# Zero-tile products around the first modulation group, and a mixer head's weights in smaller background pieces

## The chip, the cores and the metric

The kernel runs on one core of a Trainium2 chip. A core has five engines, each with its own in-order instruction queue: TensorE (PE, matrix products; PEld is its weight load), VectorE (DVE), ScalarE (ACT), GpSimd (POOL) and SyncE (SP, which here only issues transfers). The metric is the device time of one execution in microseconds, the median of several runs; lower is better.

## The reference, cut to what matters

Two layers over 256 latent tokens and 256 context tokens of width 1024. Layer 0 mixes tokens with a bidirectional mLSTM of four heads, layer 1 with latent attention; each is followed by a gated ConvFFN. Every sub-layer is modulated by columns computed from a condition vector, and ends in a LayerNorm.

```python
def _modulation(cond, w, b):
    m = jax.nn.silu(cond) @ w + b
    return jnp.split(m[:, None, :], 6, axis=-1)
...
        # one head, one chunk of the mLSTM scan
        wmat = jnp.exp(dmat - mj[..., None]) * jnp.einsum("bhjd,bhsd->bhjs", qc, kc)
        den = g * jnp.einsum("bhjd,bhd->bhj", qc, n) + jnp.sum(wmat, -1)
        h = num / jnp.maximum(jnp.abs(den), jnp.exp(-mj))[..., None]
...
    hl = _modulate(x, ml[0], ml[1])
    x = _layer_norm(ALPHA * x + ml[2] * yl, ln_g[i, 0], ln_b[i, 0])
    f = _conv_ffn(_modulate(x, ml[3], ml[4]), ...)
    x = _layer_norm(ALPHA * x + ml[5] * f, ln_g[i, 1], ln_b[i, 1])
```

## The kernel before

**Numbers in two halves.** Every fp32 operand is split into a rounded high half and the remainder, and a product is three matmuls (`mm3`, lines 383 to 385: high by high, high by low, low by high). For weights, ACT writes the high half (line 323) and DVE the low half (line 326); for activations it is lines 388 and 389. The weights stream from HBM in tiles of 128x1024 (512 KB): three buffers `raw` for what has landed, three buffers `w` for the two halves (`NRAW`, `NB`, line 32). `raw` is free for the next transfer when both halves have been written; `w` is free when the last product that reads it is done.

**The start.** `start_up` (line 584) computes the first two modulation vectors in four groups of 256 columns, interleaved with the first projection `up`. The order on PE, DVE and ACT is written out by hand in `STEPS` (line 50) and kept as it stands. `S` splits a group's modulation weights (four tiles for a group), `A` multiplies them with the condition (`ada_rows`, line 462: 16 products of 512 columns for a group, four for a tile, in the order high, low, high, low; one PSUM row `adar`), then ACT copies the row out (line 477), `T` transposes it (line 484), `M` applies it, `W` splits a tile of `up`, two digits are products of `up`. `D` issues products of a tile of zeros (`self.zero`, line 435) into a PSUM tile `idle` that nothing reads (line 659): three after `A0`, six after `T0`.

**The heads.** For head h the main line issues the query and key projection (`w_qk`, line 921: eight weight tiles, 24 products each), then `av(h-1)`, the product of the finished mixing weights with the values, then the scores `s_mm(h)`. Beside it runs background work as Python generators: every weight tile is followed by `tick`, which advances the first generator in the list by one step for each tick (two after each tile here, so 16 in a head). `post(h-2)` (line 1098) is first in the list: it squares, normalises (line 1107) and transposes (`hnT`, line 1113) the head before. `head(h-1)` (line 963) is next: masks, then for three groups of query blocks the exponentials on ACT (line 1007), their product with the scores on DVE (line 1008), the denominators `R` (1014 to 1018), and the scaled and added weights `W` (1023, 1025), then three steps of transposes `PT` (line 1037). Each of the three groups is one step. At the seventh of the eight tiles `v_load` issues the next values' transfers on POOL's queue.

**The last head** is computed beside the output projection `mout`: eight weight tiles (12 products `y` each, two ticks each), with `head(3)` and then `post(2)` as background and the values of head 3 split along the way; then `av(3)`, then the rest of `mout`. A second background list multiplies modulation weights on DVE (`junk`, line 512), with a rate of its own.

Outside `start_up` a scheduler places the instructions of each engine by the program order and its own estimate of when they can run. So a step that is issued later in Python can move other instructions too; the order that comes out is read from the built program, engine by engine.

**The end.** `ln_rows` (line 1131) normalises the two halves of the latent tokens; `nm` (line 1151) is minus the mean times the reciprocal deviation, a bias for ACT.

Of the kernel before, what the change touches and what calls it, by code (L numbers as in the profile page):

```python
# [11 lines left out]
ALU = mybir.AluOpType  # L12
# [35 lines left out]
GROUPS = ((0, 2), (2, 4), (4, 6), (6, 8))  # L48
LOADS = [(c[0], int(c[1])) for c in "a0 r0 r1 x0 r2 a1 r3 r4 x1 a2 x2 x3 a3".split()]
STEPS = [(c[0], int(c[1])) for c in (  # L50
    "S0 W0 A0 D3 T0 D6 M0 W1 W2 S1 00 01 W3 W4 A1 03 T1 M1 02 04 10 11 S2 A2 12 T2 M2 13 14 21 "
    "S3 20 A3 24 T3 22 23 M3 31 32 33 34 30").split()]

TAIL = {"mout": 4, "aout": 7, "fout1": 6}
# [300 lines left out]
class K:  # L355
# [106 lines left out]
    def ada_rows(self, g, parts):  # L462

        nc = self.nc
        f0, f1 = GROUPS[g]
        nf = f1 - f0
        n = 256 * nf
        pr = self.ps("adar")
        for i, (hi, lo) in enumerate(parts):
            for kk in range(1024 // n):  # L470
                k = i * (1024 // n) + kk
                c = slice(kk * n, (kk + 1) * n)
                for x in (hi, lo):
                    nc.tensor.matmul(pr[0:4, :n], self.condr[:, k, :], x[:, c], start=k == 0 and x is hi,
                                     stop=k == 7 and x is lo)
        r = self.s2("adarow")
        nc.scalar.copy(r[0:4, :n], pr[0:4, :n])
        return r
# [105 lines left out]
    def start_up(self):  # L584

        nc, st = self.nc, self.st
        self.hT = []
        self.xcd = self.dr.tile([16, 128, 512], F32, name="xcd")
        self.xmd = self.dr.tile([16, 128, 512], F32, name="xmd")
        self.t2d = {(n, p, j): self.dr.tile([128, 1024], F32, name="t2d")  # L590
                    for n, a, b in (("v", 2, 4), ("y", 1, 6)) for p in range(a) for j in range(b)}
        self.xA, self.x1, self.xc, self.xcr = {}, {}, [], []
        w, ps, raws = [], [], []
        src = self.a["ada_w"][0]
        self.adaw, self.xT = {}, []
        for op, g in LOADS:
            f0, f1 = GROUPS[g] if op != "r" else (0, 0)
            if op == "a":
                wd = 128 * (f1 - f0)
                nk = 512 // wd  # L600
                self.adaw[g] = []
                for k in range(8):
                    if k % nk == 0:
                        t = self.uf("adaw")
                        self.adaw[g].append(t)
                    ap = bass.AP(tensor=src.tensor, offset=src.offset + k * 128 * 6 * D + f0 * 128,
                                 ap=[[6 * D, 128], [D, 2], [1, wd]])
                    c = k % nk * 2 * wd
                    nc.sync.dma_start(t[:, c:c + 2 * wd].rearrange("p (a b) -> p a b", a=2), ap)
            elif op == "x":  # L610
                for i in range(f0, f1):
                    x = self.s2("xT")
                    nc.sync.dma_start(x, self.a["tokT"][i])
                    self.xT.append(x)
            else:
                n, _ = st.ids["up", g, 0]
                r = self.pool.tile([128, 1024], F32, tag="raw" if g < 3 else "ar", name="raw0",
                                   bufs=NRAW if g < 3 else 2)
                nc.sync.dma_start(r, st.ws[n])
                raws.append(r)  # L620

        def wsplit(m):
            if m < 3:
                t = self.pool.tile([128, 2, CW], F32R, tag="w", name="w", bufs=NB)
                h, l = t[:, 0], t[:, 1]
            elif m == 3:
                h, l = [self.pool.tile([128, CW], F32R, tag="acc", name="w0", bufs=2) for _ in range(2)]
            else:
                h, l = [self.pool.tile([128, CW], F32R, tag="u", name="w0", bufs=NU) for _ in range(2)]
            self.split(h, l, raws[m])  # L630
            w.append((h, l))
            ps.append(self.ps("up"))

        def part(g, ms):
            for m in ms:
                for k in range(*GROUPS[g]):
                    c = slice(k * 128, (k + 1) * 128)
                    self.mm3(ps[m], (w[m][0][:, c], w[m][1][:, c]), (self.hT[k][:, 0], self.hT[k][:, 1]),
                             k == 0, k == 7)

        e = mybir.EngineType
        idle = self.ps("idle")
        rows = {}
        with self.tc.manual_schedule(engines={e.PE, e.DVE, e.Activation}):
            for op, g in STEPS:
                if op == "S":
                    rows[g] = self.ada_split(g)
                elif op == "A":
                    rows[g] = self.ada_rows(g, rows[g])
                elif op == "T":  # L650
                    rows[g] = self.ada_T(g, rows[g])
                elif op == "M":
                    self.ada_cols(g, rows.pop(g))
                    self.mod_tiles(range(*GROUPS[g]))
                elif op == "W":
                    wsplit(g)
                elif op == "D":
                    for _ in range(g):
                        nc.tensor.matmul(idle, self.zero[:, 0:128], self.zero, start=True, stop=True)
                else:  # L660
                    part(int(op), [g])
        for m in range(NUP):
            self.up_evac(m, ps[m])
# [299 lines left out]
    def head(self, h, S, big=False):  # L963
        nc = self.nc
# [11 lines left out]
        for g in range(3):  # L976
# [7 lines left out]
            nd = len(jbs)  # L984
            rng = {}
            for i, t in enumerate(jbs):
                base = 256 * i if g == 0 else 0
                for d in range(2):
                    o = W[d]
                    bias = self.gcol[:, 0, t, 32 * d + h:32 * d + h + 1]  # L990
                    spans = [(t * 128, (t + 1) * 128, Am[d])]
                    if d == 0:
                        if t > 0:
                            spans.append((0, t * 128, aB[d]))
                        lo, hi = 0, (t + 1) * 128
                    else:
                        if t == 0:
                            spans.append((128, 256, aB[d]))
                        if t >= 2:
                            spans.append((0, 256, aB[d]))  # L1000
                        if t == 2:
                            spans.append((384, 512, aB[d]))
                        lo, hi = {0: (0, 256), 1: (128, 256), 2: (0, 512), 3: (0, 512)}[t]
                    if d == 1 and t == 3:
                        nc.vector.memset(o[:, 256:384], 0.0)
                    for s0, s1, src in spans:
                        nc.scalar.activation(o[:, base + s0:base + s1], src[:, s0:s1], AF.Exp, bias=bias, scale=1.0)
                    nc.vector.scalar_tensor_tensor(o[:, base + lo:base + hi], o[:, base + lo:base + hi], 1.0,
                                                   S[g][:, base + lo:base + hi], op0=ALU.mult, op1=ALU.mult,
                                                   accum_out=den[:, 2 * i + d:2 * i + d + 1])  # L1010
                    rng[i, d] = (base + lo, base + hi)
            dv = den[:, 0:2 * nd]
            R = self.tiny(4, "R")
            nc.vector.scalar_tensor_tensor(R[:, 0:2 * nd], dv, -1.0, dv, op0=ALU.mult, op1=ALU.max)
# [4 lines left out]
            for i, t in enumerate(jbs):  # L1019
# [4 lines left out]
                                        op0=ALU.mult)  # L1024
                nc.vector.scalar_tensor_tensor(W[big][:, s0:s1], W[1 - big][:, s0:s1],
                                               R[:, 2 * i + 1 - big:2 * i + 2 - big], W[big][:, s0:s1],
                                               op0=ALU.mult, op1=ALU.add)
# [103 lines left out]
    def ln_rows(self, pss, xres, gate, fin=None):  # L1131

        nc = self.nc
        self.zs = zs = []
        for t in range(2):
            z = self.uf("z")
            st = self.tiny(6 * len(pss[t]), "st").rearrange("p (a b) -> p a b", b=6)
            for i, (ps, c) in enumerate(pss[t]):
# [4 lines left out]
                                               op0=ALU.mult, op1=ALU.add)  # L1143
                nc.vector.bn_stats(st[:, i], z[:, c])
            mv = self.tiny(2, "mv")
            nc.vector.bn_aggr(mv, st)
            rs = self.tiny(1, "rs")
            nc.scalar.activation(rs, mv[:, 1:2], AF.Sqrt, bias=self.keps, scale=1.0)
            nc.vector.reciprocal(rs, rs)
            nm = self.tiny(1, "nm")  # L1150
            nc.vector.scalar_tensor_tensor(nm, mv[:, 0:1], -1.0, rs, op0=ALU.mult, op1=ALU.mult)
            fine = len(pss[1]) > 2
            if fin is not None:
                g, b, out = fin
                for c0, c1 in ((0, 512), (512, 1024)):
                    c, h = slice(c0, c1), c0 // 512
                    hc = slice(c0 - h * 512, c1 - h * 512)
                    if t or c0 == 512:
                        nc.vector.scalar_tensor_tensor(z[:, c], z[:, c], mv[:, 0:1], g[h][:, hc],
                                                       op0=ALU.subtract, op1=ALU.mult)  # L1160
# [823 lines left out]
```

## Time and profile before

| | us |
|---|---|
| runs (three) | 1384.81, 1385.51, 1386.47 |
| median | 1385.51 |
| the profiled execution, its whole time | 1386.22 |
| its span, first to last instruction | 1384.1 |
| DVE busy in the span | 1090.0 (79%) |
| ACT busy | 713.1 (52%) |
| weight loads (PEld) busy | 1123.2 (81%) |
| 16 DMA engines moved | 297.58 MB, 215 GB/s on average |

The profile is one execution. Its page gives totals; its other views give the instructions in order of time (start, duration, engine, line, operation, tiles, and in brackets how long the engine had idled and what ended that), the waits summed by who waited for whom, and the busy time of each engine in chosen stretches, with the clock that TensorE was granted (PEclk, 1.00 is full). A matmul's duration includes its way through the array, so products that follow each other closely start more often than their durations say.

### The profile page before, as it was taken

The numbers are of one execution on the slowest core, as the hardware profiler recorded it, in microseconds if no ns is written. First come the engines' busy times: TensorE is split into PE (matmuls) and PEld (weight loads), VectorE is DVE, ScalarE is ACT, GpSimd is POOL, SyncE is SP. The second block draws the span as 40 slices with busy tenths as digits, with TensorE's granted clock in tenths as the row PEclk, the third lists the DMA queues.
The fourth block names the chain that finished last, engine by engine and source line by source line (L and its number), as shares of the span: only waits on it lengthen the run. The fifth ranks groups of instructions, "written<-read, shape, count | busy, mean of one in ns | idle before, by whom it ended". The sixth has DMA issues, their size and how long they took to land.

```text
span 1384.1 us, 18592 instructions
## 1 busy us (share of the span) xinstructions
PE 1354.0 (98%) x6567; PEld 1123.2 (81%) x6567; DVE 1090.0 (79%) x1768; ACT 713.1 (52%) x1221; POOL 121.6 (9%) x215
## 2 busy tenths in 40 slices
PE   7999999999999999999999999999999999999997
PEld 3788888888788888878898888888777888888886
DVE  6598857687688697779799878668898789788873
ACT  6585534435444555364643434334637567466660
POOL 0033000011011011120002000000001001000100
PEclk9999999999999999999999999999999999999999
DMA  9689847789666364766747877646987425256750
GB/s 338 227 293 316 290 156 247 239 286 302 214 200 204 105 232 132 250 193 228 241 147 239 300 230 234 212 145 229 312 231 226 137 99 202 109 185 185 252 202 31
DMA packets 97900, 297.58 MB, mean 215 GB/s; under 512 B 12136, under 2 KB 24808, under 8 KB 97808
## 3 DMA queue, kind: packets, MB, share of 16 engines
q1 hardware_dynamic: 68672, 218.52, 47.5%
q0 software_dynamic: 17472, 57.57, 13.3%
q10 hardware_dynamic: 11664, 20.32, 4.1%
q8 instruction: 51, 0.84, 0.2%
q14 instruction: 41, 0.34, 0.1%
HBM read 262.90 MB, written 33.46 MB: 214 GB/s over the span
## 4 chain that ended last, share of the span: by engine, by line
PE 91%; DVE 5%; ACT 2%; issue 1%; DMA 0%; SPq 0%; DVEq 0%; ACTq 0%
PE fin L1320 9%; PE fin L383 6%; PE fin L384 6%; PE fin L385 6%; PE tok L383 6%; PE tok L384 6%; PE tok L385 6%; PE y L384 5%; PE y L385 5%; PE y L383 5%; PE qk L383 4%; PE qk L385 4%; PE qk L384 4%; PE up L383 2%; PE up L385 2%; PE up L384 2%
## 5 line engine op out<-in xcount | busy, mean ns | idle before, releaser
L326 DVE TENSOR_TENSOR w<-raw,w 128x1024 fp32r<-128x1024 f32 (+3 forms) x290 | 348.1, 1203 | 141.3 <-ACT w L323 140.3
L323 ACT CAST w<-raw 128x1024 fp32r<-128x1024 f32 (+3 forms) x290 | 300.4, 1037 | 306.2 <-PE tok L385 88.6
L512 DVE SCALAR_TENSOR_TENSOR junk<-ar,bc 128x1024 f32<-128x1024 f32 x128 | 156.0, 1218 | 4.9 <-ACT bc L554 2.1
L384 PE MATMUL fin<-h,w 128*128 128x512 f32 (+1 forms) x376 | 141.2, 376 | 0.0
L385 PE MATMUL fin<-h,w 128*128 128x512 f32 (+1 forms) x376 | 140.9, 375 | 0.0
L383 PE MATMUL fin<-h,w 128*128 128x512 f32 (+1 forms) x376 | 140.8, 376 | 0.1
L1320 PE MATMUL fin<-h,w 128*128 128x256 f32 (+1 forms) x640 | 113.0, 339 | 0.0
L1320 PEld LDWEIGHTS fin<-h,w 128*128 128x128 f32 x640 | 98.2, 189 | 14.7
L383 PE MATMUL qk<-xc,w 128*128 128x512 f32 x256 | 100.7, 393 | 0.0
L385 PE MATMUL qk<-xc,w 128*128 128x512 f32 x256 | 99.9, 390 | 0.0
L384 PE MATMUL qk<-xc,w 128*128 128x512 f32 x256 | 99.8, 390 | 0.0
L384 PEld LDWEIGHTS fin<-h,w 128*128 128x128 f32 x376 | 70.8, 188 | 12.9 <-DVE h L1212 0.2
L385 PEld LDWEIGHTS fin<-h,w 128*128 128x128 f32 x376 | 70.8, 188 | 12.9
L383 PEld LDWEIGHTS fin<-h,w 128*128 128x128 f32 x376 | 70.5, 188 | 13.1 <-ACT h L1211 0.3
L383 PEld LDWEIGHTS qk<-xc,w 128*128 128x128 f32 x256 | 48.1, 188 | 10.0 <-issue 0.4
L385 PEld LDWEIGHTS qk<-xc,w 128*128 128x128 f32 x256 | 48.1, 188 | 9.9
L384 PEld LDWEIGHTS qk<-xc,w 128*128 128x128 f32 x256 | 48.1, 188 | 9.7
L383 PE MATMUL up<-hT,w 128*128 128x512 f32 x128 | 50.5, 394 | 0.5 <-ACT hT L388 0.5
L384 PE MATMUL up<-hT,w 128*128 128x512 f32 x128 | 50.1, 392 | 0.5 <-DVE hT L389 0.5
L385 PE MATMUL up<-hT,w 128*128 128x512 f32 x128 | 50.1, 391 | 0.3 <-DVE w L389 0.3
L383 PE MATMUL tok<-w,hT 128*128 128x512 f32 x128 | 49.8, 389 | 0.0
L384 PE MATMUL tok<-w,hT 128*128 128x512 f32 x128 | 49.8, 389 | 0.0
(463 smaller groups left out, 3151.2 us busy)
## 6 DMA issues: line engine op xcount, KB each, us to landing
raw<-in_ws SPq DMA_DIRECT2D x287, 512.0 KB, 4.3
ar<-in_adaT SPq DMA_DIRECT2D x80, 512.0 KB, 4.6
adaw<-in_ada_w SPq DMA_DIRECT2D x32, 256.0 KB, 6.7
t2d<-raw ACTq DMA_DIRECT2D x13, 512.0 KB, 4.9
raw<-t2d SPq DMA_DIRECT2D x13, 512.0 KB, 6.3
raw<-in_ws POOLq DMA_DIRECT2D x13, 512.0 KB, 8.0
zr<-fd ACTq DMA_DIRECT2D x33, 128.0 KB, 3.9
xmd<-xr POOLq DMA_DIRECT2D x16, 256.0 KB, 5.0
```

The costliest lines, as they stand in the source:

```text
L323: k.nc.scalar.copy(h[:, :cols], src)
L326: k.nc.vector.tensor_sub(l[:, :cols], src, h[:, :cols])
L383: mm(out, w[0], x[0], start=start, stop=False)
L384: mm(out, w[0], x[1], start=False, stop=False)
L385: mm(out, w[1], x[0], start=False, stop=stop)
L512: nc.vector.scalar_tensor_tensor(o, w, 1.0, self.bc[j], op0=ALU.mult, op1=ALU.mult, accum_out=col[:, k, j:j + 1])
L1320: nc.tensor.matmul(o, a, b, start=k == 0 and i == 0, stop=k == 7 and i == 1)
```

## The change

Three edits.

1. In the hand-written order, nine zero products are put ahead of `S0`, and in group 0's `ada_rows` two more ahead of the second, third and fourth weight tile: 15 more products in all.
2. `head` yields more often: after each of the two blocks of the first group but the last, and between a group's products (line 1008) and its denominators. A head has 12 yields and not 8; the transposes are its steps 10 to 12 and not 6 to 8.
3. `nm` is left out where the final LayerNorm does not use it (the second token tile).

In the built programs PE has 15 more instructions, DVE one fewer, the other engines as many as before. Positions move only in `w_qk` of heads 1 to 3 and in the first part of `mout`: `PT` of a head comes two weight tiles later, and on DVE and ACT the weight halves stand in other places among the head's steps. In the first part of `mout` DVE's list before `post`'s scaling (line 1107) changes from the weight tiles 3, 4, 5 and 6 to the tiles 3 to 9, and from no `junk` product to two; on PE the sixteen `hnT` transposes come after tile 7's products and no longer among tile 6's, and five of tile 8's products come ahead of `av(3)`. POOL's and SP's instructions are the same, with other waits on buffers, and some modulation loads stand a place earlier on SP.

```diff
@@ STEPS
-    "S0 W0 A0 D3 T0 D6 M0 W1 W2 S1 00 01 W3 W4 A1 03 T1 M1 02 04 10 11 S2 A2 12 T2 M2 13 14 21 "
+    "D9 S0 W0 A0 D3 T0 D6 M0 W1 W2 S1 00 01 W3 W4 A1 03 T1 M1 02 04 10 11 S2 A2 12 T2 M2 13 14 21 "
@@ ada_rows
         for i, (hi, lo) in enumerate(parts):
+            if g == 0 and i:
+                for _ in range(2):
+                    nc.tensor.matmul(self.idle, self.zero[:, 0:128], self.zero, start=True, stop=True)
             for kk in range(1024 // n):
@@ start_up
-        idle = self.ps("idle")
+        idle = self.idle = self.ps("idle")
@@ head
                     rng[i, d] = (base + lo, base + hi)
+                if i < nd - 1:
+                    yield
+            yield
             dv = den[:, 0:2 * nd]
@@ ln_rows
-            nm = self.tiny(1, "nm")
-            nc.vector.scalar_tensor_tensor(nm, mv[:, 0:1], -1.0, rs, op0=ALU.mult, op1=ALU.mult)
+            if fin is None or t == 0:
+                nm = self.tiny(1, "nm")
+                nc.vector.scalar_tensor_tensor(nm, mv[:, 0:1], -1.0, rs, op0=ALU.mult, op1=ALU.mult)
```

## The prediction

> **What bounds the kernel now.** I read the page, then the stretches, then each place the change touches in order of time.
>
> ```profile
> span 1384.1 us, 18592 instructions
> PE 1354.0 (98%) x6567; PEld 1123.2 (81%) x6567; DVE 1090.0 (79%) x1768; ACT 713.1 (52%) x1221; POOL 121.6 (9%) x215
> ...
> raw<-in_ws SPq DMA_DIRECT2D x287, 512.0 KB, 4.3
> ```
> ```profile
> 490.00:550.00 60.00, 59.98 (x284) 49.85 (x283) 47.67 (x98) 30.85 (x68) 5.77 (x11) 1.00 0.52 175
> ...
> 590.00:620.00 30.00, 28.81 (x142) 23.34 (x141) 23.26 (x58) 23.03 (x49) 6.63 (x13) 1.00 0.60 187
> 620.00:640.00 20.00, 20.00 (x98) 16.74 (x97) 19.37 (x30) 10.94 (x21) 0.00 (x0) 1.00 0.67 223
> ```
>
> Columns of the stretches: length, then busy PE, PEld, DVE, ACT, POOL, then clock. PE sets the end: 98% busy, and all of 620 to 640. So a hole opened in PE ahead of such a stretch is paid in full. Heads 1 to 3 (490 to 550 is one) leave PE no hole to close. The first part of `mout` leaves 1.19 us (30.00 less 28.81); almost all of it is this wait, for tile 4's low half:
>
> ```profile
> 605.47 1.22 DVE L326 TENSOR_TENSOR w<-raw,w 128x1024 fp32r<-128x1024 f32 x1
> ...
> 606.74 0.50 PE L384 MATMUL y<-w,hn 128*128 128x512 f32 x1 [1.07 <-DVE w L326]
> ```
>
> The most this edit can give is therefore 1.07 us.
>
> **Zero products.** The start in order:
>
> ```profile
> 0.95 0.48 DVE L436 MEMSET zero<- 128x512 f32 x1
> ...
> 6.79 0.59 PE L474 MATMUL adar<-adas,condr 128*4 128x512 f32 x1 [6.79 <-ACT adas L388]
> ...
> 8.05 1.87 PE L474 MATMUL adar<-adas,condr 128*4 128x512 f32 x4 [0.67 <-DVE adas L389]
> ...
> 10.12 2.56 PE L474 MATMUL adar<-adas,condr 128*4 128x512 f32 x8 [0.20 <-DVE adas L389]
> ...
> 13.01 0.86 PE L474 MATMUL adar<-adas,condr 128*4 128x512 f32 x3 [0.33 <-DVE adas L389]
> ...
> 13.71 0.85 PE L659 MATMUL idle<-zero 128*128 128x512 f32 x3
> ...
> 15.38 0.60 ACT L572 ACTIVATE xT<-xT,mod 128x256 f32<-128x256 f32 x1 [0.90 <-DVE mod L495]
> ```
> ```profile
> 18.30 1.99 ACT L388 CAST w<-raw 128x1024 fp32r<-128x1024 f32 x2
> 20.20 3.89 ACT L388 CAST adas<-adaw 128x1024 fp32r<-128x1024 f32 x4
> 23.99 1.99 ACT L388 CAST w<-raw 128x1024 fp32r<-128x1024 f32 x2
> ```
>
> At 8.05 products start every (1.87 - 0.59) / 3 = 0.43 us, at 13.01 every (13.71 - 13.01) / 3 = 0.23. The pace doubles inside the row at 10.12. The group's last burst runs at full pace already and begins when DVE delivers the last low half. So earlier warmth has nothing left to speed up here; and after 15.38 ACT's list is nearly solid to 26, so whatever delays the group's end delays all.
>
> When is the pace full? The two drops in the profile tell:
>
> ```profile
> 4.29:7.70 3.41, 0.59 (x1) 1.00 0.97 308
> 7.70:11.11 3.41, 2.86 (x7) 1.00 1.03 380
> ...
> 605.03:608.45 3.42, 2.35 (x11) 1.00 0.95 288
> 1076.07:1079.48 3.41, 1.81 (x12) 1.00 0.00 0
> 1079.48:1082.90 3.42, 3.42 (x14) 0.50 0.00 0
> ...
> 1185.30:1188.71 3.41, 1.46 (x11) 1.00 0.00 0
> 1188.71:1192.12 3.41, 3.35 (x15) 0.50 0.00 0
> ```
>
> (Length, PE busy, clock.) Both drops last 3.41 us and start 109.23 = 32 x 3.413 apart: windows that run free. Counted back, 313 of them from 1079.48 end at 11.1, where the pace doubles. A window with 1.81 or 1.46 us busy is followed by half clock, one with 2.35 or 2.86 by full, one with 0.59 leaves it cold. (The early 1.00 is then a missing record.)
>
> The nine products start at 1.5, when the zeros are written, and fill the window to 4.29 (2.8 of 3.41): full clock from there. They end near 5, and PE waits for the same data as before until 6.79, with one product, then 8.05. The window to 7.70 has under 1 us of work, less than the 1.46 that lost the clock: cold again from 7.70. From 8.05 PE has 15 real and six zero products. To 11.11 it starts (11.11 - 8.05) / 0.43 = 7, the other 14 take 3.2: end 14.3, against 13.01 + 3 x 0.23 = 13.7. Cost 0.6. As the windows run free, other executions have the boundary elsewhere: at 10.2 the same sum gives 13.9, at 13.0 it gives 15.2, so +0.2 to +1.5. I take +0.6. If the clock held, the zeros would fit into PE's waits, for 0.
>
> The Trainium skill (TensorE: Matmul & The Clock Gate, "What's actually happening") gives such a free-running window of about 3.4 us, and has the clock fall "after ≥1 idle window". Read literally, a window with some work would keep the clock, and the cost would be 0; this trace disagrees, with drops after 1.46 and 1.81 us of work.
>
> **Heads 1 to 3.** `PT` of heads 1 and 2 now ends right ahead of `av`.
>
> ```profile
> 512.18 1.28 DVE L389 TENSOR_TENSOR PT<-PT 128x512 fp32r<-128x512 f32 x2
> ...
> 522.35 0.69 DVE L389 TENSOR_TENSOR qk<-qk 128x512 fp32r<-128x512 f32 x1 [1.12 <-ACT qk L388]
> ```
>
> `av` begins with the first `PT` group, ready a tile earlier: 12 products, 2.7 us at 0.23. In that time ACT casts a weight tile (about 1.0) and two `PT`, DVE does one weight half and the two `PT` (1.28): about 3.6 us after the tile's end, when the second group is first read at 0.9 (eight transposes) + 2.7 = 3.6. DVE had 1.12 us idle here. I take 0; two misses, each of one such `PT` row (1.28), are the upper end, and there is no hole to gain.
>
> **The first part of `mout`.** Here DVE is the second bound:
>
> ```profile
> 597.20:615.50 18.30, 18.05 (x51) 1.00 0.71 222
> ```
> ```profile
> 613.89 1.67 DVE L1107 TENSOR_SCALAR oh<-oh,ss 128x512 f32<-128x512 f32 x4
> ...
> 614.60 2.00 PE L1113 MATMUL hnT<-ident,oh 128*128 128x128 f32 x16
> ...
> 615.48 1.22 DVE L512 SCALAR_TENSOR_TENSOR junk<-ar,bc 128x1024 f32<-128x1024 f32 x1
> 616.62 1.22 DVE L326 TENSOR_TENSOR w<-raw,w 128x1024 fp32r<-128x1024 f32 x1
> ...
> 620.11 0.39 PE L383 MATMUL av<-v,PT 128*128 128x512 f32 x1
> ```
>
> Length, DVE busy: 18.05 of 18.30 us up to the end of `post`'s scaling. Tile 4's low half moves ahead of most of the head and the 1.07 us go. But three more weight halves and two `junk` now stand ahead of the scaling, each as long as the next other, 1.14 from start to start (615.48 to 616.62): 5.7 us. With no idle left but 0.25, the scaling moves from 613.89-615.5 to 619.3-621.0. PE, in order, needs it for `hnT`. What PE does before `hnT` is all of 593 to 620.11 less the transposes (1.8) and less the old hole: it is there at 620.1 - 1.8 - 1.07 = 617.2. It waits from 617.2, first for over 2 us, then at the pace of the scaling, and ends the transposes near 621.0 + 0.6 = 621.6: 1.5 later than before. That is the lower bound of the walk. The upper one has the weights' arrival in it: tile 9's `raw` buffer is tile 6's, whose low half is now done near 611; plus 4.3 to land, 1.0 to cast, and two `PT` casts behind it on ACT whose low halves DVE does before tiles 8 and 9: scaling to 622.1, transposes to 622.6, 2.5 later. I take +2.2, nearer to that end, since the transfers' 4.3 us is itself a row. Nothing later gives it back, PE being full. Outside the walk the price runs from -1.1 (no new wait) to +3.5 (`junk`'s own load late too).
>
> A wait of over 2 us and transposes at half density leave 3 to 4 us idle within 5; split over two windows that is at least 1.5 in one, about the 1.6 (3.41 - 1.81) that dropped the clock. So a cold window follows, of which PE can use two thirds: 3.41 x 2/3 x 1/2 = +1.1 (0 to 1.7).
>
> **The end.**
>
> ```profile
> 1379.38 0.15 DVE L1151 SCALAR_TENSOR_TENSOR nm<-mv,rs 128x1 f32<-128x1 f32 x1
> 1379.45 1.41 DVE L1161 SCALAR_TENSOR_TENSOR z<-z,rs,br 128x512 f32<-128x512 f32 x2
> ```
>
> `nm` stands alone on the path: -0.07.
>
> **Sum.** 0.6 + 0 + 2.2 + 1.1 - 0.07 = +3.8 on the profiled execution (span 1384.1, whole 1386.22): 1390.0. That execution lies 0.7 above the median 1385.51, so I forecast 1389.3.
>
> **Rivals.**
>
> - *The finer steps only free tile 4* (not slower). Place: DVE's list in `mout`; it decides if the scaling still ends before PE has used up tile 7, that is, if DVE does its list some 4 us faster than its rows say. The wait of 1.07 goes, the zeros cost nothing: 1385.5 - 1.1 - 0.1 = 1384.3. Against it: 18.05 busy of 18.30. Chance 0.12.
> - *The clock holds* through windows with a little work: no 0.6 and no 1.1, leaving 2.2 - 0.07 = +2.1: 1387.6. For it: 2.35 us of 3.42 were enough at 605; against it: the two drops. Chance 0.18. (The Trainium skill, TensorE: Matmul & The Clock Gate, "What's actually happening", would have it so.)
> - *`av` waits for the late `PT`* in heads 2 and 3, 1.28 each, on top: 1391.9. For it: the sum above ends level. Chance 0.12.
> - *Nothing visible*: the hole moves from tile 4 to `hnT`, the same size: 1385.5. Chance 0.10.
>
> My forecast has 0.48.
>
> **Numbers.** About 0.2% (2.8 us) is what can be told from no change: the bounds are 1382.7 and 1388.3. The forecast's own range is 1387.8 to 1391 and lies nine tenths above the upper bound (0.43); with the late `PT` (0.12) and a third of the held clock (0.06) slower has 0.61. Faster needs more than the 1.1 us that there is to gain: 0.04 for the unforeseen. The rest, 0.35, is within. The range takes in the lower rivals' centre and the late `PT`: 1384.5 to 1392.0.
>
> **What would show it.** Full pace early and 0.43 again at 8.05, the row's last product after 14; tile 4's products without a wait; a PE wait for DVE's `oh` (line 1107's instruction) at the first `hnT`, over 2 us; the scaling near 620; a half-clock window near 620; no PE wait before `av` of heads 1 and 2. It is wrong if DVE has the scaling done by 617, or if the time is under 1387.

## The result and the profile after

| | before | after |
|---|---|---|
| median, us (runs side by side) | 1385.71 (1384.68 to 1386.80, 6 runs) | 1393.59 (1392.14 to 1395.36, 6 runs) |
| ratio, 95% interval | | 1.0057 (1.0044 to 1.007) |
| the profiled execution: span, whole time | 1384.1, 1386.22 | 1390.8, 1392.56 |
| PE instructions | 6567 | 6582 |

The change costs 7.9 us where +3.8 was forecast; the time lies 1.6 us above the range. What follows goes through the profile in order of time.

The start, from the timeline of PE after (start, duration, engine, line, operation, tiles, count, in brackets the idle time before and what ended it):

```profile
1.49 4.21 PE L662 MATMUL idle<-zero 128*128 128x512 f32 x9 [1.49 <-DVE adav L447]
7.37 0.39 PE L477 MATMUL adar<-adas,condr 128*4 128x512 f32 x1 [1.67 <-ACT adas L388]
...
11.80 1.05 PE L472 MATMUL idle<-zero 128*128 128x512 f32 x2
...
16.00 0.41 PE L487 MATMUL adat<-ident,adarow 4*128 4x4 f32 x4
```

The stretches of the clock there (length, busy PE, PEld, DVE, ACT, POOL, granted clock, DMA share, GB/s):

```profile
6.24:9.65 3.41, 1.42 (x6) 0.72 (x7) 1.59 (x2) 2.09 (x2) 0.00 (x0) 1.00 1.04 344
9.65:13.07 3.42, 3.35 (x9) 1.12 (x7) 2.99 (x3) 2.80 (x3) 0.00 (x0) 0.50 1.02 396
```

The zeros win a full-pace window, it passes mostly in waiting (1.42 us busy), and the next one is at half clock, as forecast. (The nine zeros themselves take 4.21 us and end at 5.70, not near 5.) The transposes of the row start at 16.00 and not at 14.53: +1.47, of which 0.58 is the first product (7.37 against 6.79), late because ACT's first cast waited for its weights from HBM. That is one execution against one; experiment 2 compares more. In heads 1 to 3 PE keeps this shift: +1.34 and +1.36 at `av` of heads 1 and 2, and +1.44 at the first product of `mout`. The finer steps cost nothing there.

Then the first part of `mout`. PE after, and DVE after:

```profile
624.53 3.38 PE L1119 MATMUL hnT<-ident,oh 128*128 128x128 f32 x16 [6.14 <-DVE oh L1113]
627.92 0.50 PE L383 MATMUL y<-w,hn 128*128 128x512 f32 x1
...
629.18 0.40 PE L383 MATMUL av<-v,PT 128*128 128x512 f32 x1
```
```profile
620.46 1.29 DVE L389 TENSOR_TENSOR PT<-PT 128x512 fp32r<-128x512 f32 x2 [3.10 <-ACT PT L388]
621.66 1.22 DVE L326 TENSOR_TENSOR w<-raw,w 128x1024 fp32r<-128x1024 f32 x1
...
624.00 1.67 DVE L1113 TENSOR_SCALAR oh<-oh,ss 128x512 f32<-128x512 f32 x4
```

Tile 4's wait is gone, and PE waits 6.14 us for the scaling instead. The scaling starts at 624.00, or 622.5 without the start's shift, where the prediction's bounds for that start were 619.3 and 620.4 (the upper end of the scaling, 622.1, less its own 1.67). DVE itself stood idle for 3.10 us. What it waited for is read from the chain of waits of after (start, length, what):

```profile
606.78 1.15 DVE w L326
607.98 6.79 DMA raw<-in_ws
614.87 1.05 ACT w L323
...
617.31 1.28 ACT L1110
...
618.90 1.04 ACT w L323
619.94 0.49 ACT PT L388
620.46 1.29 DVE PT L389 x2
621.75 1.13 DVE w L326
622.97 1.11 DVE w L326
624.08 0.41 DVE oh L1113
624.53 3.38 PE hnT L1119 x16
```

Raw tile 8 (still as it comes from HBM) takes 6.79 us to land. ACT has its cast (614.87) ahead of two squares, the table load and square root of `post` (1110), tile 9's cast and the last two `PT` casts; all of that stands still until 614.87 (ACT after):

```profile
614.87 1.05 ACT L323 CAST w<-raw 128x1024 fp32r<-128x1024 f32 x1 [3.35 <-DMA raw<-in_ws]
```

Beside the tile run POOL's loads, and the DMA engines are full (POOL after; then the stretch in which the tile was under way):

```profile
606.09 2.17 POOL L1276 DMA_DIRECT2D xres<-in_tok  x4 [19.30 <-ACT W L1010]
608.24 0.55 POOL L1133 DMA_DIRECT2D gate<-gd  x1
610.10 0.55 POOL L1133 DMA_DIRECT2D gate<-gd  x1 [1.31 <-DVE W L1011]
610.64 0.55 POOL L1276 DMA_DIRECT2D xres<-in_tok  x1
611.38 0.55 POOL L1276 DMA_DIRECT2D xres<-in_tok  x1 [0.19 <-issue]
```
```profile
607.98:614.77 6.79, 6.79 (x35) 5.49 (x34) 6.79 (x19) 3.44 (x8) 2.44 (x5) 1.00 0.94 312
```

These are eight loads of 256 KB, six of the residual and two of the gate; the DMA engines were busy for 0.94 of the time. The clock, in its own windows after:

```profile
617.22:620.64 3.42, 1.17 (x6) 0.61 (x4) 0.32 (x3) 3.39 (x6) 1.08 (x2) 1.00 0.94 319
620.64:624.05 3.41, 0.00 (x0) 0.00 (x0) 3.41 (x6) 1.49 (x4) 0.00 (x0) 0.50 0.51 168
624.05:627.47 3.42, 2.94 (x14) 2.94 (x15) 2.76 (x7) 0.29 (x1) 0.55 (x1) 0.50 0.83 274
```

Two windows at half clock; PE works only in the second, where the 16 transposes take 3.38 us and not 2.00. `av(3)` starts at 629.18 and not at 620.11: +9.07, less five products of tile 8 that now come first (629.18 - 627.92 = 1.26), less the start's 1.47: `mout` added 6.34 us. Later the shift changes twice. A weight product that stood at 688.93 before stands at 698.08 after, 9.15 later; 0.83 of that is new waiting for its own low half. In the last products the shift is 6.82, about 2.0 of the difference because the half-clock windows at 1079.48 and 1188.71 do not occur in this execution. The span ends 6.7 longer.

### The profile page after: what moved, and what is told of

The parts are those of the page before. It is cut to its first block, busy times and chain, and to the rows that moved or that the text cites. A ratio compares the mean times of both kernels' runs of the same rounds, so it can differ in the third digit from the quotient of the medians.

```text
span 1390.8 us, 18615 instructions
## 1 busy us (share of the span) xinstructions
PE 1358.2 (98%) x6582; PEld 1126.2 (81%) x6582; DVE 1090.5 (78%) x1767; ACT 713.0 (51%) x1221; POOL 121.4 (9%) x215
## 4 chain that ended last, share of the span: by engine, by line
PE 87%; DVE 6%; DMA 3%; ACT 2%; issue 2%; SPq 0%; DVEq 0%; ACTq 0%
PE fin L1327 9%; PE fin L384 6%; PE fin L383 6%; PE fin L385 6%; PE tok L383 6%; PE tok L385 6%; PE tok L384 6%; PE y L384 4%; PE y L385 4%; PE y L383 4%; PE qk L383 4%; PE qk L385 4%; PE qk L384 4%; DMA raw<-in_ws 2%; PE up L383 2%; PE up L385 2%
```

## The experiments

A ratio is that to the kernel before, timed beside it.

**1. The parts.** The finer steps alone; all 15 zero products alone; the change with the last head in the old steps; finer steps with `post(2)` first in the last head's list.

```diff
@@ steps alone: the change without D9, the pairs and the nm edit
@@ zeros alone: the change without the yields and the nm edit
@@ last head in old steps: head(h, S, big)
+        fine = not big
-                if i < nd - 1:
+                if fine and i < nd - 1:
-            yield
+            if fine:
+                yield
@@ post first: as "steps alone", and
-        k.bg = [k.head(3, S, True), k.post(2, tt)]
+        k.bg = [k.post(2, tt), k.head(3, S, True)]
```

> The head's finer steps alone, in all four heads; no zero products, nm as before. Theory A (the last head's finer steps put three weight halves and two modulation products ahead of the scaling on DVE, PE waits for it at the transposes, and the clock falls): about +6 us on the kernel before, near 1392, with the PE wait for DVE's oh of about 6 us and a half-clock window after it. Theory B (the zero products at the start carry most of the loss): at most +2.5, near 1388. Theory C (the late transposes of heads 1 to 3): also near 1392, but with PE waits at av in 460 to 590 and none at the scaling.

> The zero products alone (nine ahead, two before each of three tiles), heads as before. Theory A: +0.6 to +1.5 us, 1386.2 to 1387.2, with the last modulation product of the group after 14 us and slow products again after 8 us. Theory B: +5 or more, over 1390. If the products only fill waits: 1385.6.

> The changed kernel whole, but the last head (beside the output projection) in the old coarse steps; heads 0 to 2 keep the finer ones. Theory A: as the zero products alone, 1386.2 to 1387.2, and the scaling again near 614 plus the start's delay. Theory C: near 1392 still. If heads 0 to 2 cost 1 us each: 1388 to 1389.

> The finer steps alone, and in the output projection's first part the background list has the post step of head 2 first and head 3 behind it, so that the scaling is issued early. Theory A: the wait for the scaling is gone, and with it the fall of the clock; tile 4's wait is gone as well: 1384.5 to 1385.6. If the head's transposes come too late for av(3) instead: PE waits there, 1387 to 1390. If the finer steps cost by their number and not by the scaling's place: near 1392.

| | median, us | ratio, 95% interval |
|---|---|---|
| steps alone | 1392.52 | 1.0044 (1.0032 to 1.0056) |
| zeros alone | 1388.09 | 1.0010 (1.0001 to 1.0018) |
| last head in old steps | 1386.08 | 0.9996 (0.9987 to 1.0004) |
| `post(2)` first | 1389.22 | 1.0024 (1.0016 to 1.0033) |

The finer steps are the cost: without the zeros they give the long wait (5.39 us before `hnT`, raw tile 8 landing in 6.14). Only those of the last head matter: with them taken back the change costs nothing, so those of heads 0 to 2 are free. (That kernel keeps all fifteen zeros, so their 0.1% lies at the edge of what these runs can tell.) With `post(2)` first the wait before `hnT` is gone, but `PT` is then late: `av(3)` runs from 619.75 to beyond 631 among `y` products, with a wait of its own (PE of that kernel):

```profile
600.70 2.17 PE L1116 MATMUL hnT<-ident,oh 128*128 128x128 f32 x16
...
630.00 0.50 PE L383 MATMUL av<-v,PT 128*128 128x512 f32 x1 [1.44 <-ACT PT L388]
```

So that kernel moves the wait rather than removes it.

**2. The zero products apart.** The nine alone; the six between the bursts alone; seventeen in place of nine.

```diff
@@ nine alone (on the kernel before)
-    "S0 W0 A0
+    "D9 S0 W0 A0
@@ seventeen (on the change)
-    "D9 S0 W0 A0
+    "D17 S0 W0 A0
```

> The nine zero products at the start alone, added to the kernel before. Theory (free windows): they win a full-pace window that PE spends waiting for data, and the row's burst from about 8 us runs at half pace as before, so nothing is gained; nothing is added to the row either, as the nine end near 5.5, before the first data product. Time within 0.5 us of before (1385.5 to 1386.5 on a like chip). Rival: the products delay the group by themselves (PE still busy with them when the first data lands, or the half-pace window now falls on the row's last burst): +0.7 to +1.5, the last row product past 14. Rival: the clock holds and the row ends before 13.2: -0.3 to -0.5.

> The six zero products between the four bursts of the first row alone, added to the kernel before. Theory: in the half-pace window each pair takes 0.85 us of PE, the first two pairs fit partly into PE's waits (0.67, 0.20 and 0.33 us before), the row's last product starts 0.5 to 1.0 us later than before (13.47 to about 14.2), time +0.5 to +1.0. Rival: PE has room for the pairs in its waits and the row's end does not move (within 0.2): the delay seen with both edits came from the nine products or from the later landing of the first weights (the start of the first data product after 7.2).

> The changed kernel with seventeen zero products at the start in place of nine: eight more of about 0.23 us each at full pace, so that PE is busy from 1.5 to near 7 and the window that decides has well over 2.3 us of work. Theory (the clock is kept by the work in each free window): the half-clock window that began at 9.65 does not come, the row's products run at 0.23 apart from the first data product on, the row is bound by the split of the weights on ACT and DVE, its last product starts near 13.5 and not 14.9, and the time is 0.7 to 1.5 us under the changed kernel's. Rival: the clock falls anyway within two windows of its release: last row product at 14.5 to 15.5, time within 0.5 us of the changed kernel's. Rival: the zeros themselves delay the first data product past 7.6: time equal or up to 0.7 us more.

The nine: 1386.08, 1.0000 (0.9991 to 1.0009); the row's transposes at 14.62 (before 14.53). The six: 1387.38, 1.0008 (0.9999 to 1.0017); transposes at 15.45, although the first product came early, at 6.50. The row varies between executions, though: in the eight traces without any of these zeros its transposes start at 14.53 to 15.11 (mean 14.88), in the seven with all fifteen at 15.05 to 16.11 (mean 15.56). So the fifteen cost about 0.7 us, and 14.53, with which the single traces are compared, is the earliest of all. By these traces the six are late and the nine are not; as time the interval of the six just includes no cost. Seventeen in the change: 1393.70, 1.0058 (1.0046 to 1.0071), no better than nine. The row was still at half pace until 11.45, so more zeros ahead of the data did not hold the clock; this trace lacks most of their records, so how full the window before was cannot be read.

**3. The late tile.** The four residual loads of the context half are held back until the last tile of the first half of `mout` is split (a one-element copy on ACT writes into their buffers first).

```diff
-    def res_load(self, src, t0):
+    def res_load(self, src, t0, late=False):
                 x = self.s2("xres")
+                if late:
+                    self.gate(x[0:1, 0:1])
...
-        xr = k.res_load(tokr, 0)
+        xr = k.res_load(tokr, 0, True)
```

> The changed kernel, with the four residual loads of the context half (256 KB each, on POOL's queue) held back until the last weight tile of the first part of mout is split, so that they no longer share the DMA engines with the raw tile 8. Theory (the tile's landing is what I mis-sized): raw tile 8 lands about 4 to 4.5 us after its issue and not 6.8, ACT's cast of it no longer waits (or under 1 us), post's scaling starts 1.5 to 2.7 us earlier (from 622.3 to 619.6..620.8), PE waits 3.4 to 4.6 us before the first hnT and not 6.1, and av(3) starts 2 to 3 us earlier, more if only one half-clock window follows and not two. Time 1389.5 to 1392 against 1393.6. Rival (DVE's list sets it, not the landing): the scaling moves by less than 0.7 and the time stays at 1393 to 1394. Rival (the landing is late for another reason, other transfers on the engines): the landing still takes over 6 us.

In the trace the theory holds, and more than that. (The expectation's 622.3 is wrong: the scaling of after starts at 624.00.) Tile 8 is cast 3.7 us after its issue without waiting for its transfer, the scaling starts at 619.98, and the chain of waits there has no transfer left in it, only DVE's list:

```profile
616.44 1.29 DVE PT L389 x2
617.73 1.13 DVE w L326
618.95 1.11 DVE w L326
620.06 0.41 DVE oh L1113
620.51 3.58 PE hnT L1119 x16
```

The time is not as expected (1389.5 to 1392) but as before this edit: 1393.92, 1.0062 (1.0048 to 1.0075). The profiled run shows one place where part of the gain is given back, the first transposes `zT` of the next LayerNorm, where the changed kernel had no wait. In the chain of waits a raw tile is now under way for 9.62 us there, since all the residual loads issue at 636.83 to 641.88:

```profile
666.57 0.33 PE L1206 MATMUL zT<-ident,z 128*128 128x128 f32 x1 [1.94 <-DVE z L1179]
```
```profile
643.81 9.62 DMA raw<-in_ws
```

The profiled run is the fastest of the five (1391.24); where the others lose the rest is not shown.

**4. DVE's list or the tile?** `mout`'s first eight tiles without `junk` products: as it was built, that takes one `junk` and one weight half out of DVE's list ahead of the scaling. Once alone, once with the loads held back as in 3.

```diff
-            k.outmm("mout", range(i, i + 1), hn, pc, 0, 16, 2, n2=ADA_M)
+            k.outmm("mout", range(i, i + 1), hn, pc, 0, 16, 2, n2=0)
```

> The changed kernel with the background list of modulation products (junk) stopped through the first part of mout; the built program then has one junk and one weight half fewer on DVE ahead of post's scaling (2 x 1.14 us), and no other difference of order on PE there. Theory (the scaling is held by the late raw tile 8, whose cast stands ahead of the square root and the last PT casts on ACT): the landing is as late as before, the DVE list only gets shorter behind it by the weight half: scaling 1.0 to 1.3 us earlier, PE's wait before the first hnT 4.8 to 5.2 instead of 6.1, time 1392 to 1393. Rival (DVE's list alone): scaling 2.3 us or more earlier, PE's wait under 4 us.

> Both at once: residual loads of the context half held back and no junk products in the first part of mout. Theory: with the tile on time DVE's list sets the scaling, and every entry taken from it counts: against the kernel with late residual loads alone the scaling comes another 2.0 to 2.4 us earlier, PE's wait before the first hnT falls from 3.1 to 0.7 to 1.1 us, and the clock stays at full there (the window would keep over 2.4 us of work). The later collision of the residual loads with the next weight tiles (about 2 us at the first zT) stays, so time 1388.5 to 1391. Rival (something else holds the scaling, such as ACT's square root or PT casts): PE's wait stays over 2 us.

| | raw tile 8 | scaling, less the start's shift | wait before `hnT` | ratio, 95% interval |
|---|---|---|---|---|
| the change | 6.79 | 624.00 - 1.47 = 622.5 | 6.14 | 1.0057 (1.0044 to 1.007) |
| shorter list | 6.68 | 620.52 - 0.52 = 620.0 | 3.93 | 1.0053 (1.004 to 1.0067) |
| loads held back | 3.7 or less | 619.98 - 0.53 = 619.45 | 3.08 | 1.0062 (1.0048 to 1.0075) |
| both | no wait | 618.62 - 1.58 = 617.04 | 1.00 | 1.0046 (1.003 to 1.0061) |

The shorter list has the rival's numbers (2.5 us earlier, 3.93), though the tile was as late as ever. My expectation overlooked that tile 8's half now stands ahead of the last two `PT` low halves, where DVE had stood idle, and tile 9's behind the scaling: 2 x 1.13 us less between tile and scaling. With the tile on time the same edit gains 2.4. So lateness and list add up: the scaling waits for the tile, and then for what DVE has behind it. With both gone, no half-clock window follows at `hnT`. The time shows less of it: 1392.12 for both, where 1388.5 to 1391 was expected, and 1393.85 for the shorter list alone, whose profiled run lost over 3 us between 1004 and 1018, two windows at half clock among it. In these two kernels what the wait at `hnT` gives back is hardly seen in the time.

**5. One step.** The kernel before with a single extra yield in the last head, with and without the `junk` products.

```diff
+        last = big
         full = {0: [(0, 0)...
...
                     rng[i, d] = (base + lo, base + hi)
+                if last and i < nd - 1:
+                    yield
```

> The kernel before with one extra yield in the last head alone (between the two blocks of the first group): its DVE list ahead of the scaling has one weight half and two junk products more than before, hnT comes after one product of tile 8. Theory (the price goes with the length of the list ahead of the scaling): scaling some 3.4 us later than before (first one near 617.3), PE there near 617.4, so hnT waits under 1 us and then runs at the scaling's pace; tile 4's wait of 1.07 goes. Time within 1 us of before, 1385.5 to 1387 on a like chip, no half-clock window there. Rival (any extra step in the last head brings the long wait): hnT waits over 3 us, time over 1389.

> The same single yield without junk products in the first part of mout: one weight half more ahead of the scaling than in the kernel before, hnT among tile 7's products. Theory: tile 4's wait (1.07 us) goes and the scaling, about 1.1 us later, is still in time for hnT: 0.5 to 1.1 us under before. Rival: the wait of tile 4 turns up again at hnT: within 0.3 us of before. Rival: the junk products put off are missed later, at the modulation columns that need them, by a wait of over 1 us: slower than before.

My theory fell here. One step costs 4.3 us: 1390.77, 1.0033 (1.002 to 1.0046). The chain of waits is the one of after, with a raw tile in it. PE (below) waits 0.22 us before tile 5's products and then 3.25 at `hnT`:

```profile
605.33 7.01 DMA raw<-in_ws
612.44 1.05 ACT w L323
```
```profile
609.53 0.50 PE L384 MATMUL y<-w,hn 128*128 128x512 f32 x1 [0.22 <-DVE w L326]
621.02 3.46 PE L1116 MATMUL hnT<-ident,oh 128*128 128x128 f32 x16 [3.25 <-DVE oh L1110]
```

Without `junk`: 1390.41, 1.0023 (1.0013 to 1.0034), the wait before `hnT` 1.68, and later waits that the kernel before does not have (0.31, 0.76 and 0.46 us between 690 and 711). The length of DVE's list is thus not the whole price. The chain points to the order on ACT: a cast of a tile on its way stands ahead of `post`'s square root, and ACT waits 4.41 us for that tile. Experiment 6 tests this.

**6. The loads where there is room.** The same four residual loads held back until tile 8 is split (the first issues at 624 to 628), for one step, for the change, for the kernel before, and for one step without `junk`.

```diff
-        k.outmm("mout", range(8, 12), hn, pc, 0, 16, 1, n2=ADA_M)
-        k.drain()
+        k.outmm("mout", range(8, 9), hn, pc, 0, 16, 1, n2=ADA_M)
         tokr = a["tok"].rearrange("(t p) d -> t p d", p=128)
-        xr = k.res_load(tokr, 0)
+        xr = k.res_load(tokr, 0, True)
+        k.outmm("mout", range(9, 12), hn, pc, 0, 16, 1, n2=ADA_M)
+        k.drain()
```

> The kernel before with one extra yield in the last head, and the four residual loads of the context half held back until tile 8 of mout is split (about 628). Theory (the late raw tile on ACT's list made the wait of 3.25 us there, not the step itself): ACT's cast no longer waits 4.4 us for its tile, the scaling starts 2.5 to 4 us earlier (617 to 618), PE waits under 1 us before hnT, no half-clock window follows, and the time is 3 to 5 us under the one-step kernel's 1390.8: 1385.5 to 1388. Rival (the step alone, through the longer DVE list): scaling moves by under 1 us, time over 1389.5.

> The changed kernel with the same four residual loads held back until tile 8 is split. Theory: at hnT as with the loads held back to the end of mout (PE's wait near 3.1 us and not 6.1, one half-clock window at most), but no wait of about 2 us at the first zT, since the loads now run at 628 to 640: 2.5 to 4 us under the changed kernel, 1389.5 to 1391.5. That would be the time that my sum gave (1389.3). Rival (the loads collide with some weight tile wherever they run): over 1392.5.

> Control: the same move of the residual loads in the kernel before. Theory: its casts of tiles 6 and 7 did not wait for their raw tiles in the stretch that PE needs, so nothing but at most tile 4's wait (1.07) can be had: within 0.5 us of before, or up to 1 us less. Rival (the residual loads cost time wherever the weights stream): 1.5 us or more under before.

> One extra yield in the last head, no junk products in the first part of mout, and the residual loads held back as above. Theory: scaling near 614.5 to 616, no wait before hnT and none for tile 4; what is left is the cost of the junk products put off (2 to 3 us in later waits, as without the held-back loads): 1386 to 1389. Rival: the later waits came from the residual loads too: 1384 to 1385.5, under before.

| with the loads moved | median, us | ratio, 95% interval | not moved |
|---|---|---|---|
| the change | 1389.39 | 1.0026 (1.0017 to 1.0035) | 1.0057 (1.0044 to 1.007) |
| one step | 1386.04 | 0.9996 (0.9987 to 1.0004) | 1.0033 (1.002 to 1.0046) |
| one step, no `junk` | 1386.53 | 1.0000 (0.9992 to 1.0009) | 1.0023 (1.0013 to 1.0034) |
| the kernel before | 1386.57 | 1.0003 (0.9994 to 1.0011) | 1 |

The loads' move is worth nothing in the kernel before, over 4 us in the change and with one step, and 3 to 4 us with one step and no `junk`. With one step ACT then waits 1.13 us for its tile and not 4.41, the scaling starts at 617.14 and not at 620.49, and PE's wait is nearly gone:

```profile
617.67 2.06 PE L1116 MATMUL hnT<-ident,oh 128*128 128x128 f32 x16 [0.35 <-DVE oh L1110]
```

Without `junk` as well, PE has no wait before `hnT`. The change with the loads moved, chain of waits and PE:

```profile
611.95 3.49 DMA raw<-in_ws
615.54 1.05 ACT w L323
...
617.11 1.29 DVE PT L389 x2
618.40 1.13 DVE w L326
619.62 1.11 DVE w L326
620.73 0.41 DVE oh L1113
```
```profile
621.18 2.06 PE L1119 MATMUL hnT<-ident,oh 128*128 128x128 f32 x16 [3.06 <-DVE oh L1113]
623.48 0.50 PE L383 MATMUL y<-w,hn 128*128 128x512 f32 x1 [0.23 <-ACT hn L1122]
```

This is the walk of the prediction, through tile 9 and its cast (3.49 us to land, where it had put 4.3): `av(3)` starts at 624.73, +4.62, less 1.25 for the five products and 1.22 for the start: +2.15, where +2.2 was forecast. That the time, 1389.39, is nearly the forecast 1389.3 is partly luck: this trace has no half-clock window at `hnT`, for which the sum held 1.1, and 1.22 at the start, for which it held 0.6. No version is measurably faster than the kernel before.

## Why the prediction failed

- **Direction and place: right.** PE's wait moved from tile 4 to `hnT`, behind DVE's longer list; tile 4's 1.07 us went; heads 1 to 3 cost 0.
- **The term that was mis-sized: the `mout` stall, +2.2.** The failed step is "plus 4.3 to land": a median over 287 transfers, put in for a transfer that runs beside eight of POOL's. That walk was moreover for tile 9 and held no wait for tile 8. Tile 8, whose cast stands ahead on ACT, took 6.79 us, and ACT kept the square root and the `PT` casts behind it. The change with the loads moved gives 2.15 for the term; the stall in `mout` of the change, without its clock loss, is 6.34 - 1.3 = 5.0. So the late tile added about 3 us, as the scalings of the two show too: 624.00 less 620.64, less 0.25 between their starts, is 3.1. The upper price outside the walk (+3.5, "`junk`'s own load late") looked at the wrong load. The profile of before shows the residual loads in this very stretch, and they were not read:

```profile
601.46 2.17 POOL L1269 DMA_DIRECT2D xres<-in_tok  x4 [11.37 <-ACT W L1007]
```

They alone did not foretell the lateness. The raw tile that before issued at 606.71, 3 us behind these four, landed in 4.2 us. In the change the four, which by the trace wait for ACT's `W`, start at 606.09, and tile 8 is issued among them at 607.98.

The Trainium skill would have warned of this step (DMA: Bandwidth & Descriptors, "Issuing engines are not separate DMA queues"): transfers issued by any engine run on the same 16 DMA engines and interleave. The runs agree: 6.79 us beside POOL's loads, 3.7 or less with them held back.
- **The clock, +1.1: nearly right.** The transposes took 3.38 us and 2.06 at full clock: +1.3. There were two cold windows and not one, but the first held no work.
- **The zeros, +0.6: about right.** The mechanism (a window won and lost again, pairs at half pace) is as forecast. The trace of after has +1.47, 0.58 of it from late first weights, which vary from run to run (first product at 6.50 to 7.81 in the traces here); the mean over the traces is +0.7. The zeros alone measured +0.1%.
- **`nm`, -0.07:** too small to be measured, and not tried alone.
- **The rivals.** "The finer steps only free tile 4" and "nothing visible" are refuted by the wait's row (6.14 us), "`av` waits" by PE's shift, which does not grow at `av` (+1.34 and +1.36). "The clock holds" is refuted by the windows for the change; it is what the profiled run with the loads moved shows at `hnT`.

## What to carry to other kernels

A transfer on the path of a stall is priced by what will share the DMA engines with it when it is issued, on every queue, and not by the median of the page. Before delaying a step of background work, look for casts of weights still on their way that stand ahead of small instructions (a square root, a table load) which another engine needs: an in-order queue passes the lateness on, as here 3.35 us of waiting on ACT became 3.10 us idle on DVE. A load that is moved out of the way may be paid again where it lands beside other transfers; try more than one place.

## What the runs showed of the hardware

How much work keeps the clock is not a plain threshold on PE's busy time in a window, as far as that time can be read (the ends of products in it are modelled). In the windows ahead of a drop PE was busy 1.81 and 1.46 us (before), 1.17 and 1.42 (after); but in the change with the loads moved, windows with 2.12 and 1.65 us in sequence kept full clock around the same wait:

```profile
616.00:619.41 3.41, 2.12 (x8) 1.40 (x8) 3.37 (x5) 1.63 (x4) 0.00 (x0) 1.00 0.65 205
619.41:622.83 3.42, 1.65 (x14) 1.52 (x15) 3.42 (x8) 1.33 (x3) 0.00 (x0) 1.00 0.87 266
622.83:626.24 3.41, 3.18 (x16) 2.50 (x15) 3.35 (x6) 2.33 (x4) 0.00 (x0) 1.00 0.39 143
```

The Trainium skill (TensorE: Matmul & The Clock Gate, "What's actually happening") has the cold state come after an idle window; here it came after windows with up to 1.81 us of work, and after one with 1.65 the clock stayed full. What else decides stays open. The phase of the windows differs between executions, so a wait of 3 us may cost a half-clock window (620.51 with the loads held back to the end: transposes 3.58 us) or none (621.18 with the loads moved: 2.06).
